# Linear attention on one core: two stores of the first pair moved behind the last load

## The chip, the cores and the metric

The kernel runs on one core of a Trainium2 chip. The metric is the device time of one execution in microseconds (us); each time given is that of whole executions, and one further execution was taken with the hardware profiler.

## The reference

Linear attention with the feature map relu(x) + 1, for 8 batches x 12 heads = 96 heads, 512 rows of 64 numbers each, float32 in and out:

```python
Q_feat = np.maximum(0, Q) + 1
K_feat = np.maximum(0, K) + 1
KV = np.einsum('bhkd,bhkv->bhdv', K_feat, V)
K_sum = np.sum(K_feat, axis=2)
numerator = np.einsum('bhqd,bhdv->bhqv', Q_feat, KV)
denominator = np.einsum('bhqd,bhd->bhq', Q_feat, K_sum)
return (numerator / (denominator[:, :, :, None] + 1e-10)).astype(np.float32)
```

Each of Q, K, V and the output has 12.58 MB in float32.

## The kernel before

The heads are handled in six "pairs", s = 0 to 5; a pair is two blocks n = 0, 1 of 128 partitions x 32 rows of 64. For each pair the kernel loads K, V and Q (2 MB of float32 each, turned into 1 MB of bfloat16 by the transfer itself), computes, and stores 2 MB of float32.

The order of work is not left to a scheduler. The dictionary ORDER lists, for every engine, its tasks in the order in which the engine is to run them. A task's name is a letter, the pair, and what part of the pair it is:

- `lv5`, `lk5`, `lq5`: the loads of V, K and Q of pair 5, issued by POOL (line 131). The loads of pairs 0 and 1 are issued ahead of the lists; the very first K block is loaded on SP into a buffer of the output pool (line 124).
- `f50`, `f51`: K's features of the two blocks on DVE (line 147). `v502`: V's block 0, quarter 2, copied into a block diagonal form by DVE or ACT (line 159). `q5`: Q's features on DVE (line 167).
- `k`: the matmuls of features with V and ones (line 178); `e`: their results copied from PSUM by ACT (lines 192 and 196); `t`: transposes of Q's features (line 202); `c`: those copied from PSUM by ACT (line 207).
- `m40` to `m47`: the output matmuls of pair 4 in eight parts (line 219); `n40` to `n47`: for each part a reciprocal and a multiplication on DVE, which write the output tile `o_sb` (lines 235 and 236).
- `s40`, `s41`: the stores of pair 4 in two halves of 1 MB, the first behind n40 to n43, the second behind n44 to n47 (line 138). Pairs 0 to 4 are stored from POOL. Pair 5 is stored from SP as `s50` (1 MB), `s51` and `s52` (half of that each).

What a task waits for is taken from the buffers. K, V and Q have two buffers each, so lv5 waits until all copies `v3..` have read V of pair 3. The output tiles rotate over four buffers, and the first K block took one of them ahead of pair 0; the output tile of pair 4 stands where that of pair 0 stood, and that of pair 5 where that of pair 1 stood. The first norm of pair 4 in DVE's list is n41, the first of pair 5 n50:

```python
return [("om", s, at[0])] + [("st", s - OUT_BUFS, j) for j in stores_of(s - OUT_BUFS)]
```

The parts of the three lists that the text refers to are, in order (DVE's around the last two pairs):

```
DVE  ... q4 f41 n27 n30 n31 n32 n33 f50 n34 v501 n35 f51 n36 n37 v513 v510 n41 n40 q5 n43 n42 ...
POOL ... lk4 lv4 lq4 s00 lv5 lk5 s01 lq5 s10 s11 s20 s21 s30 s31 s40 s41
SP   s50 s51 s52
```

Of the kernel before, what the change touches and what calls it, by code (L numbers as in the profile page):

```python
# [41 lines left out]
        e40 v500 c43 e41 v511 v512 c42 c50 e50 c51 e51 c53 c52  # L42
    """,
    POOL="""
        lv2 lk2 lq2 lv3 lq3 lk3 lk4 lv4 lq4 s00 lv5 lk5 s01 lq5 s10 s11 s20 s21 s30 s31 s40 s41
    """,
    SP="""
        s50 s51 s52
# [371 lines left out]
```

## Time and profile before

| what | value |
|---|---|
| median of 3 runs | 125.86 us (125.64 to 125.92) |
| profiled execution | 125.95 us |
| its span, first to last instruction | 124.2 us |
| busy in the span | DVE 93.5 us (75%), PE 82.6 (67%), ACT 74.3 (60%), POOL 25.2 (20%) |
| read from and written to HBM | 37.75 MB and 12.58 MB |

Busy time is that of the engines' instructions; the DMA engines, sixteen of them, have a row of their own in the slices, and a table of issues with the time from issue to landing. Adding that time to an issue's start gives the moment at which the transfer has landed. A wait for several things is put down to the one that came last by the profile, and where the named engine had long been done, it was another, often a transfer.

### The profile page before, as it was taken

Reading aid. Unit: us, or ns where it says so; the run is one execution under the profiler, and the core shown is the slowest. Engines: PE = TensorE matmul, PEld = TensorE weight load, DVE = VectorE, ACT = ScalarE, POOL = GpSimd, SP = SyncE. Lnnn points to the kernel's source line nnn. Section 1 sums busy time; section 2 is a strip of 40 time slices with the busy share of each in tenths; the row PEclk is TensorE's granted clock in tenths of the full one; section 3 lists DMA queues with packets and bytes.
Section 4 is the critical chain, followed back from the end, with each engine's and each line's share of the span. In section 5 each row is a group of like instructions: output and inputs, shape, how many; then the busy total and the mean of one; then the engine's idle time right before and its main releaser. Section 6 shows DMA issues by size and latency. Waiting matters only on the chain.

```text
span 124.2 us, 2353 instructions
## 1 busy us (share of the span) xinstructions
PE 82.6 (67%) x960; PEld 62.0 (50%) x960; DVE 93.5 (75%) x188; ACT 74.3 (60%) x94; POOL 25.2 (20%) x52
## 2 busy tenths in 40 slices
PE   0000099983999896879439999978577999955000
PEld 0000077862767774568326777856375667633000
DVE  4799963459589696995979799999389999799200
ACT  7538000575756999929991299953999955930000
POOL 6991042000005100073000391202200202020000
PEclk9999999999599999999995999999999999997555
DMA  3999999999999999999999999999999999999992
GB/s 95 333 214 214 215 212 212 215 214 216 214 215 214 212 214 215 215 215 215 215 212 214 215 215 277 310 199 214 277 318 227 389 414 417 416 414 416 408 406 107
DMA packets 8731, 32.13 MB, mean 259 GB/s; under 512 B 528, under 2 KB 528, under 8 KB 8592
## 3 DMA queue, kind: packets, MB, share of 16 engines
q0 software_dynamic: 7504, 28.84, 94.5%
q1 hardware_dynamic: 1216, 3.15, 6.7%
q8 instruction: 7, 0.11, 0.3%
q14 instruction: 4, 0.03, 0.1%
HBM read 37.75 MB, written 12.58 MB: 405 GB/s over the span
## 4 chain that ended last, share of the span: by engine, by line
DMA 39%; DVE 20%; PE 13%; ACT 12%; POOL 6%; issue 2%; POOLq 0%; ACTq 0%
DMA q_raw<-in_Q_dram 20%; DMA k_raw<-in_K_dram 18%; DVE o_sb L236 9%; ACT v_all L159 8%; PE kva_ps L178 7%; DVE kf L147 4%; PE o_ps L219 3%; DVE v_all L159 3%; ACT qt L207 3%; DVE recip L235 2%; DVE qf L167 2%; POOL kva L383 2%; PE qt_ps L202 2%; POOL v_raw L131 2%; POOL q_raw L131 1%
## 5 line engine op out<-in xcount | busy, mean ns | idle before, releaser
L178 PE MATMUL kva_ps<-v_all,kf 128*128 128x260 bf16 x384 | 54.6, 294 | 22.6 <-DVE v_all L159 17.6
L178 PEld LDWEIGHTS <-kf 128*128 128x128 bf16 x384 | 37.4, 104 | 33.2 <-DVE v_all L159 18.2
L159 ACT COPY v_all<-v_raw 32x2048 bf16<-32x2048 bf16 x19 | 36.0, 1896 | 7.6 <-DVE recip L235 3.5
L236 DVE TENSOR_TENSOR o_sb<-o_ps,recip 128x512 f32<-128x512 f32 x48 | 33.2, 692 | 1.7
L207 ACT COPY qt<-qt_ps 128x1024 bf16<-128x1024 bf16 x24 | 23.8, 1014 | 9.4 <-PE qt_ps L202 9.1
L219 PE MATMUL o_ps<-kva,qt 128*64 128x130 bf16 x384 | 20.5, 232 | 5.7 <-DVE o_sb L236 4.1
L147 DVE TENSOR_SCALAR kf<-k_raw,shift,least 128x2048 bf16<-128x2048 bf16 x22 | 16.8, 808 | 9.5 <-PE kva_ps L178 5.2
L159 DVE COPY v_all<-v_raw 32x2048 bf16<-32x2048 bf16 x29 | 20.1, 692 | 0.8
L219 PEld LDWEIGHTS <-qt 128*64 128x64 bf16 x384 | 12.9, 112 | 14.0 <-DVE o_sb L236 5.8
L192 ACT CAST kva<-kva_ps 64x256 bf16<-64x256 f32 x24 | 8.9, 372 | 17.9 <-PE kva_ps L178 17.5
L202 PE MATMUL qt_ps<-identity,qf 128*128 128x128 bf16 x192 | 14.7, 221 | 3.6 <-ACT qt L207 2.5
L202 PEld LDWEIGHTS <-qf 128*128 128x128 bf16 x192 | 12.0, 98 | 5.1 <-issue 2.6
L138 POOL DMA_DIRECT2D out_dram<-o_sb x10 | 8.0, 805 | 30.2 <-DVE recip L235 15.6
L131 POOL DMA_DIRECT2D v_raw<-in_V_dram x7 | 4.8, 684 | 39.7 <-DVE recip L235 18.0
L167 DVE TENSOR_SCALAR qf<-q_raw 128x1024 bf16<-128x1024 bf16 x24 | 8.8, 432 | 5.1 <-DMA q_raw<-in_Q_dram 5.1
L235 DVE RECIPROCAL recip<-o_ps 128x8 f32<-128x8 f32 x48 | 9.6, 201 | 2.6 <-PE o_ps L219 2.3
L131 POOL DMA_DIRECT2D k_raw<-in_K_dram x6 | 4.2, 700 | 12.9 <-DVE kf L147 12.9
L131 POOL DMA_DIRECT2D q_raw<-in_Q_dram x6 | 5.1, 858 | 1.2 <-DVE qf L167 1.2
L261 DVE MEMSET v_all<- 128x2600 f32 x2 | 4.5, 2225 | 1.1 <-issue 1.1
L196 ACT CAST kva<-kva_ps 64x4 bf16<-64x4 f32 x24 | 4.1, 169 | 0.0
L262 ACT COPY v_all<-zero 128x1560 f32<-128x1560 f32 x2 | 2.9, 1488 | 0.0
L147 DVE TENSOR_SCALAR kf<-o_sb,shift,least 128x2048 bf16<-128x2048 f32 x2 | 2.6, 1340 | 0.0
(18 smaller groups left out, 6.6 us busy)
## 6 DMA issues: line engine op xcount, KB each, us to landing
out_dram<-o_sb POOLq DMA_DIRECT2D x10, 1024.0 KB, 22.5
q_raw<-in_Q_dram POOLq DMA_DIRECT2D x6, 1024.0 KB, 23.9
k_raw<-in_K_dram POOLq DMA_DIRECT2D x5, 1024.0 KB, 19.5
v_raw<-in_V_dram POOLq DMA_DIRECT2D x5, 1024.0 KB, 18.3
o_sb<-in_K_dram SPq DMA_DIRECT2D x1, 1024.0 KB, 4.9
v_raw<-in_V_dram POOLq DMA_DIRECT2D x2, 512.0 KB, 8.6
out_dram<-o_sb SPq DMA_DIRECT2D x1, 1024.0 KB, 8.5
out_dram<-o_sb SPq DMA_DIRECT2D x2, 512.0 KB, 7.5
```

The source lines that it names most:

```text
L131: nc.gpsimd.dma_start(out=t[:, ns[0] : ns[-1] + 1], in_=drams[x][:, 2 * s + ns[0] : 2 * s + ns[-1] + 1])
L138: engine.dma_start(out=o_dram[:, 8 * s : 8 * s + 8][:, ms], in_=outs[s][:, ms], single_packet=engine is nc.gpsimd,)
L147: nc.vector.tensor_scalar(out=kf[:, :, a], in0=raw["k", s, n], scalar1=shift[:, a : a + 1], scalar2=least[:, a : a + 1], op0=ALU.add, op1= ...
L159: copy(out=v_alls[n][ps, :, b * D : b * D + D], in_=raw["v", s, n][ps])
L167: nc.vector.tensor_scalar(out=qf[:, :, cs, n], in0=rows[:, :, cs], scalar1=1.0, scalar2=1.0, op0=ALU.add, op1=ALU.max,)
L178: nc.tensor.matmul(kva_pss[s, n], lhsT=kfs[s, n][:, c].rearrange("p a d -> p (a d)"), rhs=v_alls[n][:, c], start=(c == 0), stop=(c == ROWS ...
L192: nc.scalar.copy(out=kva[po, a::2, n, 0:D], in_=kva_ps[pi, 0 : 4 * D].rearrange("p (b d) -> p b d", b=4),)
L202: nc.tensor.transpose(qt_ps[:, c, r], qfs[s][:, r, 2 * i + c], identity)
L207: copy(out=qts[s][:, 2 * i : 2 * i + 2], in_=qt_pss.pop((s, i)).rearrange("p c r q -> p c q r"),)
L219: nc.tensor.matmul(o_ps[64 * t : 64 * t + 64, c // 2, (c % 2) * W : (c % 2) * W + W], lhsT=qts[s][:, 4 * i + c, 16 * k : 16 * k + 16], rhs ...
L235: nc.vector.reciprocal(out=recip, in_=cells[:, :, :, :, D:D1])
L236: nc.vector.tensor_tensor(out=outs[s][:, e + 2 * u :: 4, 4 * i : 4 * i + 4].rearrange("p n (b c) d -> p b c n d", b=2), in0=cells[:, :, :, ...
```

## The change

In POOL's list, s00 and s01, which stood between lq4 and lv5 and between lk5 and lq5, are placed behind lq5. Nothing else is touched: the same instructions with the same tiles are issued, on the same engines.

```diff
     POOL="""
-        lv2 lk2 lq2 lv3 lq3 lk3 lk4 lv4 lq4 s00 lv5 lk5 s01 lq5 s10 s11 s20 s21 s30 s31 s40 s41
+        lv2 lk2 lq2 lv3 lq3 lk3 lk4 lv4 lq4 lv5 lk5 lq5 s00 s01 s10 s11 s20 s21 s30 s31 s40 s41
     """,
```

## The prediction

> **What bounds the kernel now.** I read the page's slices first, then the chain, then the transfers one by one with their landings, and last the timelines of POOL, SP and DVE around the moved stores.
>
> The slices of the page: each digit is the busy share of a fortieth of the span (3.1 us), the numbers are GB/s.
>
> ```profile
> DVE  4799963459589696995979799999389999799200
> DMA  3999999999999999999999999999999999999992
> GB/s 95 333 214 214 215 212 212 215 214 216 214 215 214 212 214 215 215 215 215 215 212 214 215 215 277 310 199 214 277 318 227 389 414 417 416 414 416 408 406 107
> ```
>
> No compute engine is full throughout, but the DMA engines are, from the second slice to the last but one. The rate has two levels: about 214 GB/s for loads (counted as bf16 written, so twice that is read) and about 415 for stores. Between them, in slices 25 to 31, the two moved stores stand among the loads of the last pair.
>
> The chain of waits tells another story: its last piece is DVE's last norm, and before it come ACT, PE and DVE without a break from 62.8 us on.
>
> ```profile
> 114.85 0.69 DVE o_sb L236
> ```
>
> It ends at 115.5 us, 8.7 us short of the span's end. So I ask what happens after it: the issues of the SP queue, from DMA queries over 112:117, with the time from issue to landing in the last column.
>
> ```profile
> out_dram<-o_sb SPq DMA_DIRECT2D x1, 1024.0 KB, 8.5
> out_dram<-o_sb SPq DMA_DIRECT2D x2, 512.0 KB, 7.5
> ```
>
> The last store, s52, is asked for at 115.6 and takes 7.7 us, landing at 123.3. Its neighbour s51 (asked for at 114.73, 7.3 us) lands at 122.0, so the bytes of s52 need 1.3 us; the other 6.4 us it stands behind older stores. On the page the very first K load, on the same queue with next to nothing ahead, took 4.9 us for 1024 KB from issue to landing. The slack of the last store therefore lies between 7.7 - 4.9 = 2.8 and 7.7 - 1.3 = 6.4 us. The end is set by bytes waiting at the DMA engines, not by the chain.
>
> **The two moved stores.** POOL's timeline around them, then its DMA issues between 69.5 and 73.2 us in the order of time (last column again issue to landing).
>
> ```profile
> 55.08 0.73 POOL L131 DMA_DIRECT2D q_raw<-in_Q_dram  x1
> 55.78 1.10 POOL L138 DMA_DIRECT2D out_dram<-o_sb  x1
> 70.32 0.70 POOL L131 DMA_DIRECT2D v_raw<-in_V_dram  x1 [13.43 <-issue]
> 71.02 0.72 POOL L131 DMA_DIRECT2D k_raw<-in_K_dram  x1
> 71.73 0.79 POOL L138 DMA_DIRECT2D out_dram<-o_sb  x1
> 72.50 0.79 POOL L131 DMA_DIRECT2D q_raw<-in_Q_dram  x1
> ```
>
> ```profile
> v_raw<-in_V_dram POOLq DMA_DIRECT2D x1, 1024.0 KB, 15.3
> k_raw<-in_K_dram POOLq DMA_DIRECT2D x1, 1024.0 KB, 19.5
> out_dram<-o_sb POOLq DMA_DIRECT2D x1, 1024.0 KB, 21.3
> q_raw<-in_Q_dram POOLq DMA_DIRECT2D x1, 1024.0 KB, 25.4
> ```
>
> Start plus last column is the landing: v5 at 85.6, k5 at 90.5, s01 at 93.0, q5 at 97.9. The same query for q4 (55.08 + 22.4) and s00 (55.78 + 24.5) gives 77.5 and 80.3. Transfers of POOL's queue land in the order of issue, one after the other: a load alone costs 90.5 - 85.6 = 4.9 us, a store 93.0 - 90.5 = 2.5.
>
> **The change part by part.** Nothing is added or removed: ten stores and the same loads still go through POOL, with 2 x 1 MB of stores behind lq5 instead of among the loads.
>
> *POOL's own time.* lv5 is held until 70.32 by the release of its buffer: DVE's copies for the third block of V end at 69.8. That stays. With s00 gone from 55.78, POOL idles 14.5 us instead of 13.4. Then lv5, lk5, lq5 go out at 70.3, 71.0 and 71.7, s00 and s01 at about 72.5 and 73.3 (0.8 us each by the rows at 71.73 and 73.29), s10 at about 74.1 instead of 73.29, s11 0.8 later too. These wait in the queue for 27 us and more anyhow; s20, asked for at 78.06, is far behind them. Cost 0, hidden by that backlog.
>
> *Does the queue run dry without s00?* q4 lands at 77.5, v5 is asked for at 70.3: 7.2 us of transfers stand ahead. Cost 0; it would begin to cost if lv5 were released after about 76.
>
> *The loads.* Counting on from 77.5: v5 lands at 82.4 (3.2 us earlier), k5 at 87.3 (3.2), q5 at 92.2 (5.7).
>
> *The two stores.* s00 lands at 94.7 (14 us later), s01 at 97.2 by nominal durations, or 97.9 if the sum of these five transfers stays as measured. From s10 on (100.5) the queue stands where it stood. This is the main term: the same five transfers between 77.5 and 97.9, in another order, 0 us.
>
> *Compute.* DVE's timeline shows whom the earlier loads free:
>
> ```profile
> 87.38 0.69 DVE L236 TENSOR_TENSOR o_sb<-o_ps,recip 128x512 f32<-128x512 f32 x1
> 90.56 1.53 DVE L147 TENSOR_SCALAR kf<-k_raw,shift,least 128x2048 bf16<-128x2048 bf16 x2 [2.50 <-DMA k_raw<-in_K_dram]
> 99.42 0.69 DVE L236 TENSOR_TENSOR o_sb<-o_ps,recip 128x512 f32<-128x512 f32 x1
> ```
>
> The 2.50 us wait of f50 for k5 goes (87.3 is before 88.1, when DVE is free). ACT's wait of 3.50 us before v502, ended at 85.75, is put down to DVE's recip, but v5 landed at 85.6, so that also shrinks to about 0.5. Compute of the last pair moves 2.5 us forward.
>
> *A wait added.* The line at 99.42 is n41, the first norm of pair 4. Its output tile takes the buffer of pair 0 (four rotate, and the first K load took one), so it waits for s00 and s01 to land. Before, s01 was in at 93.0 and n41 did not wait. Now it would come at 99.42 - 2.5 = 96.9 and waits until 97.2 to 97.9: 0.3 to 1.0 us. Behind it on DVE stand n40, q5, n43 and all the rest; PE's m42 and later m's wait for the psum they free, and t50 for q5. Net, DVE still runs 1.5 to 2.2 us earlier.
>
> *What that buys.* s52 would be asked for 1.5 to 2.2 us earlier and find the same bytes ahead of it: it waits 1.5 to 2.2 us longer. Gain 0.
>
> The sum: 0 on the profiled execution (span 124.2, 125.95 with what lies around it). The median of the runs shown is 125.86, 0.09 below, and the forecast is put on it.
>
> **Rivals.** *Faster: alternating between stores and loads costs engine time, and three of the four changes of kind go.* From q4 to v5, s00 + v5 took 85.6 - 77.5 = 8.1 us where 2.5 + 4.9 = 7.4 are nominal: 0.7 too much. From k5 to q5, s01 + q5 took 97.9 - 90.5 = 7.4: nothing too much. So the price is between 0 and 0.7 for the first alternation and 0 for the second. A landing is that of the slowest of 16 engines, and a hiccup of some of them in one execution looks the same; one alternation in two without any cost speaks for the hiccup. Time: 125.86 - 0.7 = 125.16 if all of it is systematic and on the engines that end last, 125.6 at a third.
>
> *Slower: the hold at n41 decides.* It does so if s01 lands so late that the last store loses its slack: n41 may start at 99.42 + 2.8 by the lower bound of the slack, 102.2, at no cost. s01 would have to land 4 to 5 us behind 97.9, that is, with two further transfers served ahead of it. At s01 landing with s10's place and s11's (102.9), the price is 102.9 - 102.2 = 0.7: 126.6. The landings in order of issue speak against it.
>
> *Slower: SP's stores meet more of POOL's.* SP's s50 (asked for at 112.21) lands at 120.7. While it was pending, POOL's s40 landed at 104.27 + 11.5 = 115.8 and s41 at 108.92 + 10.1 = 119.0: 3.2 us for s41 in place of 2.5, and then s50 only 1.7 behind. From s31 (98.04 + 15.0 = 113.0) to s50, three stores took 7.7 us against 7.5. So mixing cost 0.2 net, 0.7 if nothing were given back. With s50 asked for up to 2.2 us earlier nearly one more store mixes: another 0.1 to 0.7, and 126.0 to 126.6. I take the lower end, since 1.7 shows the time given back.
> The Trainium skill, page "DMA: Bandwidth & Descriptors", section "Queues, rings and completion order", says that an engine takes turns between the queues it has work for, a whole packet at a time. By that rule mixing only trades one store's delay for another's, and this rival gives 0 on the sum; the pair 3.2 and 1.7 agrees, and nearer to no cost than to 0.7.
>
> *The change does nothing in the trace:* excluded by the timeline, since POOL issues in the order written.
>
> **How the numbers follow.** The forecast (queue full, 0) gets 0.60, with 125.6 to 126.1 as its own range, since the runs shown lie 0.28 apart. Alternation gets 0.22, at 125.2 to 125.6. The n41 hold gets 0.06 and the mixing, above its lower end, 0.12, both at 126.1 to 126.6. A measurement of this kernel can tell about 0.2%, 0.25 us, from no change; so faster 0.22, same 0.60, slower 0.18. The range takes most of the alternation's prices and most of the mixing's: 125.3 to 126.4.
>
> **What would show it.** Right: v5, k5, q5 land near 82.4, 87.3 and 92.2; the slices show a clean step from 214 to 415 GB/s near 92 us with no mixed ones; f50's 2.50 us are gone; n41 waits for a store for up to 1.0 us; DVE's last norm ends 1.5 to 2.2 us earlier while s52 takes about 9.5 us to land; span 124.2. Wrong: a span that follows DVE's end, a DMA row with a digit below 9 between 10 and 120 us, s01 landing far from 97.2 to 97.9, or a stretch from q4's to s10's landing that isn't 23 us.

## The result and the profile after

The changed kernel takes 125.46 us (median of 22 runs, 125.28 to 125.67), the kernel before 125.72 us beside it (22 runs, 125.42 to 126.66). The ratio is 0.9975, 95% interval 0.9964 to 0.9985: 0.25% faster. The time lies in the predicted range, but the forecast "no effect" does not hold, since the interval leaves out 1.

The slices of the changed kernel, as they were shown of before:

```profile
DVE  4799962449589696995969889999999896997000
DMA  3999999999999999999999999999999999999993
GB/s 101 333 215 212 212 215 216 214 214 216 215 212 214 214 216 212 214 218 214 218 215 214 214 214 212 215 212 215 216 314 419 413 421 415 410 417 415 411 409 143
```

The mixed slices are gone: loads at about 214 GB/s run up to slice 29, and within slice 30 the rate steps to about 415. The DMA engines are still busy from one end to the other. DVE ends earlier, in slice 37.

POOL's timeline, and the DMA issues of POOL between 69.5 and 72.3 us (last column: issue to landing):

```profile
55.00 0.72 POOL L131 DMA_DIRECT2D q_raw<-in_Q_dram  x1
70.24 0.72 POOL L131 DMA_DIRECT2D v_raw<-in_V_dram  x1 [14.52 <-issue]
70.95 0.72 POOL L131 DMA_DIRECT2D k_raw<-in_K_dram  x1
71.67 0.72 POOL L131 DMA_DIRECT2D q_raw<-in_Q_dram  x1
72.38 3.35 POOL L138 DMA_DIRECT2D out_dram<-o_sb  x4
```

```profile
v_raw<-in_V_dram POOLq DMA_DIRECT2D x1, 1024.0 KB, 12.1
k_raw<-in_K_dram POOLq DMA_DIRECT2D x1, 1024.0 KB, 16.3
q_raw<-in_Q_dram POOLq DMA_DIRECT2D x1, 1024.0 KB, 20.5
```

Start plus last column: v5 lands at 82.3, k5 at 87.3, q5 at 92.2, against 82.4, 87.3 and 92.2 in the prediction. DVE's timeline at f50 and at n41:

```profile
87.44 0.69 DVE L236 TENSOR_TENSOR o_sb<-o_ps,recip 128x512 f32<-128x512 f32 x1
88.05 1.62 DVE L147 TENSOR_SCALAR kf<-k_raw,shift,least 128x2048 bf16<-128x2048 bf16 x2
97.36 0.69 DVE L236 TENSOR_TENSOR o_sb<-o_ps,recip 128x512 f32<-128x512 f32 x1 [0.41 <-DMA out_dram<-o_sb]
```

f50 no longer waits; n41 now waits 0.41 us for a store. The chain of waits, whose first line below starts at s01's issue (73.36) and ends at its landing, 97.24, goes through that wait and ends with DVE's last norm at 113.48, 2.1 us earlier than before:

```profile
73.36 23.88 DMA out_dram<-o_sb
97.24 0.03 issue
97.27 0.05 DVEq L236
97.32 0.04 issue
97.36 0.69 DVE o_sb L236
...
112.79 0.69 DVE o_sb L236
```

And the stores of SP, which land at the end:

```profile
out_dram<-o_sb SPq DMA_DIRECT2D x1, 1024.0 KB, 9.9
out_dram<-o_sb SPq DMA_DIRECT2D x2, 512.0 KB, 8.9
```

s51 and s52 are asked for 2.1 us earlier and take 8.9 us (the middle of the two) in place of 7.5. So 1.4 of the 2.1 us were given back, as the queue is still full; 0.7 us were not. The span went from 124.2 to 123.5 us. Compute came early exactly as worked out, and the DMA engines were faster by 0.7 us in these two executions, 0.26 us in the medians.

Where? Each landing has 16 signals in the trace, and the last of them counts. q4's last signal came at 77.52 us before and at 77.44 here, s10's at 100.45 (73.29 + 27.2) and at 99.80. From q4 to s10 that is 22.4 us against 22.9, for the same six transfers. From s10 to s52 it is 22.8 us in both. In this pair of profiles the loss of the kernel before lies between q4 and s10.

### The profile page after: what moved, and what is told of

The parts are those of the page before. It is cut to its first block, busy times and chain, and to the rows that moved or that the text cites. A ratio compares the mean times of both kernels' runs of the same rounds, so it can differ in the third digit from the quotient of the medians.

```text
span 123.5 us, 2353 instructions
## 1 busy us (share of the span) xinstructions
PE 82.7 (67%) x960; PEld 62.0 (50%) x960; DVE 93.5 (76%) x188; ACT 74.3 (60%) x94; POOL 25.0 (20%) x52
## 4 chain that ended last, share of the span: by engine, by line
DMA 54%; DVE 13%; ACT 9%; issue 6%; PE 5%; POOL 4%; POOLq 0%; DVEq 0%
DMA q_raw<-in_Q_dram 35%; DMA out_dram<-o_sb 19%; DVE o_sb L236 7%; ACT v_all L159 5%; DVE qf L167 3%; ACT qt L207 2%; PE kva_ps L178 2%; PE o_ps L219 2%; PE qt_ps L202 1%; DVE recip L235 1%; ACT kva L192 1%; POOL v_raw L131 1%; DVE kf L147 1%; POOL k_raw L131 1%; POOL out_dram L138 1%
## 5 line engine op out<-in xcount | busy, mean ns | idle before, releaser
L219 PE MATMUL o_ps<-kva,qt 128*64 128x130 bf16 x384 | 21.0, 235 | 6.7 <-DVE o_sb L236 4.6
## 6 DMA issues: line engine op xcount, KB each, us to landing
out_dram<-o_sb POOLq DMA_DIRECT2D x10, 1024.0 KB, 22.3
```

The costliest lines, as they stand in the source:

```text
L219: nc.tensor.matmul(o_ps[64 * t : 64 * t + 64, c // 2, (c % 2) * W : (c % 2) * W + W], lhsT=qts[s][:, 4 * i + c, 16 * k : 16 * k + 16], rhs ...
```

## What was tested

Three theories at first. **H**: a store ahead of v5's load holds up some of the 16 DMA engines (the 0.7 us between q4 and v5 in the profile of before). **A**: every return from a store to a load costs the same. **C**: the gain comes from compute that ends earlier.

**Half of the change, each half alone, and the order of kinds without the early compute.**

```diff
-lv4 lq4 s00 lv5 lk5 s01 lq5 s10        before
+lv4 lq4 lv5 lk5 s01 lq5 s00 s10        e1_s00_only
+lv4 lq4 s00 lv5 lk5 lq5 s01 s10        e2_s01_only
+lv4 lq4 lq5 lv5 lk5 s00 s01 s10        e3_compute_late
+lv4 lq4 s00 s01 lv5 lk5 lq5 s10        e4_both_ahead
```

> Only s00 is moved behind lq5; s01 stays between lk5 and lq5. The change as a whole gave a ratio of 0.9975 (0.9964 to 0.9985). Theory H (engines lose time where a store stood ahead of v5's load: in the profile of before the slowest of the 16 lost 0.7 us between q4's landing and v5's, none between k5's and q5's): this edit alone gives all of it, 0.9975, and the profile shows q4's to v5's landing at 4.9 us. Theory A (each change between stores and loads costs the same): half, 0.9987. Theory C (the gain comes from compute that ends earlier, not from the DMA order): v5 and k5 land early as with the whole change, so 0.9975 too; e3 tells C from H.

Measured: 1.0007 (0.9990 to 1.0023).

> Only s01 is moved behind lq5; s00 stays ahead of lv5. Theory H: nothing, 1.000, and the profile again shows more than 7.4 us from q4's landing to v5's. Theory A: half of the gain, 0.9987. Theory C: v5 and k5 land as late as before, compute ends as late, 1.000.

Measured: 1.0002 (0.9989 to 1.0016). Neither half alone gives a gain that can be told from 0. H falls with e1, and A fails in both: half the gain, 0.9987, lies below both intervals.

> As the changed kernel, but POOL asks for lq5 ahead of lv5 and lk5. The DMA engines see the same kinds in the same order (three loads, then the stores), but k5 lands at 92.2 us in place of 87.3, so f50 waits until then, later than before the change (90.5), and compute ends some 1.7 us later than before. Theories H and A: ratio to before 0.9975, since only the order of kinds counts. Theory C: no gain, 1.000 or above.

Measured: 0.9974 (0.9963 to 0.9985). Its DVE timeline at f50 and at the last norm, then SP's issues:

```profile
92.27 1.54 DVE L147 TENSOR_SCALAR kf<-k_raw,shift,least 128x2048 bf16<-128x2048 bf16 x2 [3.54 <-DMA k_raw<-in_K_dram]
117.21 0.69 DVE L236 TENSOR_TENSOR o_sb<-o_ps,recip 128x512 f32<-128x512 f32 x1
```

```profile
out_dram<-o_sb SPq DMA_DIRECT2D x1, 1024.0 KB, 5.6
out_dram<-o_sb SPq DMA_DIRECT2D x2, 512.0 KB, 4.5
```

f50 waits 3.54 us and compute ends at 117.9, 4.4 us later than in the changed kernel and 2.4 later than before, and the whole gain is there. C falls. So compute may end at least 2.4 us later than in the kernel before at no cost; the slack of its last store was put at 2.8 to 6.4.

> s00 and s01 both ahead of lv5, so one stretch of 2 MB of stores between q4 and v5, and loads without a break after it. Theory H: the loss at v5 stays, 1.000. Theory A: one change of kind to stores and back is gone of two, 0.9987. Theory C: v5 and k5 land 2.5 us later than before and compute ends later: 1.000 or above.

Measured: 1.0012 (0.9994 to 1.0030): no part of the gain, with both stores in one stretch.

So it is the order of kinds at the DMA engines, and not their number of changes: one store or two, one return or two, all give the time of before.

**More returns, the cut alone, another place, and the kernel before once more.** Theory S kept the price on returns, but let the slowest engine's delay add up only a little; F put it on the first store of the kernel; P on what else runs at 75 to 81 us.

```diff
-lk4 lv4 lq4 s00 lv5 lk5 s01 lq5 s10                  before
+lk4 lv4 s00 lq4 s02 lv5 s01 lk5 s03 lq5 s10          e5_four_alternations (512 KB each)
+lk4 lv4 lq4 lv5 lk5 lq5 s00 s02 s01 s03 s10          e6_split_behind      (512 KB each)
+lk4 s00 lv4 lq4 lv5 lk5 lq5 s01 s10                  e7_early_s00
```

> The two stores of pair 0 are cut into four of 512 KB, and one stands between each two of lv4, lq4, lv5, lk5, lq5: four returns from store to load in place of two, the same bytes ahead of q5 as before. Theory S (each return from store to load holds up some of the 16 engines by 0.2 to 0.9 us, unevenly, and the end is that of the slowest engine, so one return costs 0.3 us and more returns add a little): ratio to before 1.001 to 1.003, slow load packets behind every return. Theory F (only the first store of the kernel does it): 1.000, slow packets around the first return alone.

Measured: 1.0006 (0.9986 to 1.0025). By its centre, four returns cost no more than one (1.0007 and 1.0002 above), but the interval does not exclude the 1.001 to 1.003 of theory S. In its packets, those of loads that took over 0.33 us (0.32 is the rule) lie between 69 and 72 us, ahead of the first of the four stores; the later returns show almost none. v4, the load ahead of that store, lands 5.29 us after k4 by the mean of the 16 signals, in place of 4.9 in the changed kernel. That fits theory F, but r1, below, shows slow packets near its second store too, so F is not settled either.

> The control of the one before: the same four stores of 512 KB, all behind lq5. Theories S and F: as the changed kernel, 0.9975. If the cut itself costs something, it shows here.

Measured: 0.9971 (0.9953 to 0.9989): the cut costs nothing, and all behind lq5 the gain is there.

> One return from store to load, but ten us earlier: s00 between lk4 and lv4, landing near 70 us; s01 behind lq5. Theories S and F: the loss of one return, 1.000. Theory P (the loss at 75 to 81 us belongs to what compute or POOL do there): none, 0.9975.

Measured: 1.0017 (0.9999 to 1.0036). P falls: at another place the loss is there too.

> The kernel before, unchanged: a second profile of it, and what two equal kernels differ by. All theories: 1.000. If the 0.7 us lost between q4's and v5's landing was a chance of one execution, load packets near 81 us are not slow here; by S and F they are again.

Measured: 1.0001 (0.9981 to 1.0020). Its profile again has slow load packets near 75 and 81 us, and near 94 too. The 0.7 us between q4 and v5, though, are not there: by POOL's starts and its landings, q4 came at 55.05 + 22.9 = 78.0 and v5 at 70.66 + 14.7 = 85.4, 7.4 us in all. From q4 to s10 the last engine took 22.9 us again. The loss of the slowest engine thus falls between other transfers from one execution to the next, and what a pair of landings shows of it is chance.

**Form of the stores, queue, or writing to HBM.** M: writes to HBM among reads from it cost 0.3%, once. K: the form of POOL's stores. Q: any break in POOL's stream of loads.

```diff
-            single_packet=engine is nc.gpsimd,
+            single_packet=engine is nc.gpsimd and s > 0,     e8_many_packets (order of before)
```

> The kernel before, with the order of before, but the two stores of pair 0 without the single_packet option, so that the order of kinds stays and only the form of the stores changes. Theory M (HBM writes among HBM reads cost 0.3 to 0.5 us at the slowest engine, once, however many there are): 1.000. Theory K (it is the form of POOL's stores, one packet for each engine, that breaks the stream of loads): 0.997.

Measured: 1.0003 (0.9980 to 1.0025). K falls as far as this option goes; the trace lists the same 7040 packets of 4 KB on POOL's queue with and without it, so it does not show that the form of the stores changed.

```diff
+    def copy_aside():
+        nc.gpsimd.dma_start(out=scratch, in_=outs[0][:, 0::2], single_packet=True)
...
+lk4 lv4 lq4 x00 lv5 lk5 lq5 s00 s01      e9_copy_among   (x00: the copy)
+lk4 lv4 lq4 lv5 lk5 lq5 x00 s00 s01      e10_copy_behind, e14_copy_behind
+lk4 x00 lv4 lq4 lv5 lk5 lq5 s00 s01      e13_copy_early
+lk4 lv4 x00 lq4 lv5 lk5 lq5 s00 s01      e15_copy_mid
+lk4 lv4 s00 lq4 lv5 lk5 lq5 s01          e16_store_mid   (no copy)
```

> The changed kernel (s00, s01 behind lq5) with one more transfer that the result does not use: 1 MB of pair 0's output copied from SBUF to SBUF, on POOL's queue ahead of lv5, where s00 stood. It adds its own time in this kernel and in its control, so the two are compared with each other. Theory M: equal to the control, since nothing is written to HBM among the loads. Theory Q (any transfer of another kind in the stream of loads costs this): 0.003 above the control.

> The control of the one before: the same copy behind lq5. An estimate from the change's rows, a store of the same size at 2.5 us: ratio to before 0.9975 + 0.020 = 1.017, and by theory M the same in the run before, by theory Q 1.020 there.

Measured: 1.0183 (1.0141 to 1.0224) and 1.0173 (1.0134 to 1.0212). The difference, 0.001, can't be told from 0 nor from 0.003.

> The changed kernel once more, beside the same runs of the kernel before as the other three, and for a second profile. All theories: 0.9975; by M no load packet is held up between the landings of q4 and of k5.

Measured: 0.9980 (0.9957 to 1.0002). The centre agrees with the first comparison; this interval alone would not exclude 1. Much as M has it, none of POOL's packets between 74 and 82 us took over 0.33 us, in this profile as in the first one of the changed kernel; in the two profiles of the kernel before 20 and 14 did.

> The added copy from SBUF to SBUF now between lk4 and lv4, where a single store gave 1.0017 (0.9999 to 1.0036); both stores of pair 0 behind lq5. Theory M: equal to its control. Theory Q: 0.003 to 0.004 above it.

> The control of the one before, run beside it: the same copy behind lq5; it was at 1.0173 (1.0134 to 1.0212). Theories M and Q: 1.0175.

Measured: 1.0214 (1.0189 to 1.0239) and 1.0178 (1.0159 to 1.0197): 0.0036 apart by their centres, as Q has it, though with 6 and 4 runs the two intervals overlap a little. The stretch in which k4 is loaded, just ahead of the copy, first of e13, then of its control (busy time of PE, PEld, DVE, ACT and POOL, then PE's clock, the DMA engines' busy share and their rate in GB/s):

```profile
64.00:67.00 3.00, 2.35 (x20) 1.64 (x21) 2.93 (x7) 1.71 (x2) 0.00 (x0) 0.76 1.03 208
```

```profile
64.00:67.00 3.00, 2.48 (x17) 1.51 (x18) 2.93 (x7) 1.54 (x2) 0.00 (x0) 0.50 1.08 217
```

208 against 217 GB/s would be 27 KB in these 3 us, but the same view has 215 and 209 GB/s, the other way round, for 62 to 64 us, so the rates alone show little. The packets show more. In e13, 26 of POOL's packets between 64 and 68 us took over 0.33 us, 5.8 us in all above 0.324 each; in the control none did. By the mean of its 16 signals k4 lands 5.30 us after k3 in e13 and 4.91 in the control. So loads are held up just ahead of the copy, with no write to HBM anywhere near.

> The added copy from SBUF to SBUF at a third place, between lv4 and lq4; both stores of pair 0 behind lq5. With the copy behind lq5 the ratio was 1.0178 (1.0159 to 1.0197). Theory M (writes to HBM needed): 1.018. Theory Q (any break in POOL's stream of loads costs): 1.021.

Measured: 1.0186 (1.0159 to 1.0214): by its centre 0.001 above the control, again not to be told from either theory.

> The store s00 at the same place, s01 behind lq5. Theories M and Q: the loss of one break, 1.000 to 1.002. If the place decides, 0.9975.

Measured: 1.0040 (1.0019 to 1.0061), 0.0065 above the changed kernel: by its centre, a store at this place costs more than at the other places on POOL's queue, and more than M or Q expected.

```diff
-SP   s50 s51 s52
+SP   s00 s50 s51 s52          e11_s00_on_SP   (POOL: lq5 s01 s10)
+SP   s00 s01 s50 s51 s52      e12_both_on_SP  (POOL: lq5 s10)
```

> s00 is asked for by SP as soon as its four norms are done (near 40 us), on SP's own queue, so that POOL's queue holds an unbroken stream of loads; s01 stands behind lq5 as in the changed kernel. Theory M (it is writes to HBM among reads from it): the loss is there, 1.000, with slow load packets near 41 us. Theory Q (it is the break in POOL's queue): no loss, 0.9975.

Measured: 0.9999 (0.9987 to 1.0010). The loss is there with POOL's stream of loads unbroken, so a break in it is not needed. (SP's stores go without single_packet, in packets of 2 KB in place of 4, so the queue is not all that differs.) The slow packets that M looked for near 41 us are not there, though. The DMA queries over 38:60 show the store spread thin among the loads:

```profile
out_dram<-o_sb SPq DMA_DIRECT2D x1, 1024.0 KB, 18.1
```

It takes 18.1 us to land, as the loads beside it go on.

> s00 and s01 both from SP's queue, near 40 and 46 us; no store of pair 0 is left on POOL's queue. Theory M: 1.000, since a second store among the loads costs nothing more. Theory Q: 0.9975.

Measured: 1.0033 (1.0014 to 1.0052). M's "nothing more" is wrong for SP's queue: the second store costs another 0.0034. Here s51 and s52 took 4.3 us to land (the middle of the two), a little less than e3's 4.5, and compute ended at 119.4, so some of it may be the late compute.

**What all profiles together show.** Each transfer's landing is told by 16 signals, as many as there are DMA engines, and they are taken here as one from each. The table has s52's, counted from the mean landing of v3 (ahead of anything moved), as mean of the 16 and as the last, for one profiled execution each:

```
                        mean    last   (us since v3's mean)
after                   69.90   70.61
r2_after                69.87   70.83
e3_compute_late         69.92   70.57
e6_split_behind         69.88   70.69
before                  70.13   71.15
r1_before               70.06   71.01
e1_s00_only             70.00   70.98
e2_s01_only             70.02   70.96
e4_both_ahead           70.17   71.00
e5_four_alternations    70.20   71.17
e7_early_s00            70.02   70.84
e8_many_packets         69.95   70.79
e16_store_mid           69.95   71.43
e10 / e14 copy_behind   72.37 / 72.37   73.26 / 73.17
e9 copy_among           72.39   73.15
e13 copy_early          72.74   73.87
e15 copy_mid            72.58   73.80
```

With the loads unbroken the last engine ends at 70.57 to 70.83. With a store of POOL's among them it ends at 70.79 to 71.43 (mean of the nine: 71.04, against 70.68 for the four): 0.36 us. The mean over the engines differs by 0.16 us, from 69.89 to 70.06. e16 weighs in this: without it the last engine's difference is 0.31 us. So about half of the loss is work held up, and the other half is unevenness between the engines. The end of the kernel is the last engine's.

The held-up packets account for the mean. Between 62 and 95 us, POOL's packets that took over 0.33 us cost 5.5 and 3.5 us in all above 0.324 each in the two profiles of the kernel before, and 1.1 and 0.6 us in the two of the changed kernel. Shared by 16 engines, the difference is 0.23 us on average, beside 0.21 between the means of these four rows.

e11 and e12 are not in the table, since their stores land beside the loads around v3. Counted from v2's mean landing, s52's mean comes at 84.66 to 84.72 us in the four with unbroken loads, at 85.05 in e11 and at 85.68 in e12. On SP's queue the loss is thus in the mean too.

Beside the stores, the unevenness has a source that is in every profile alike:

```profile
q8 instruction: 7, 0.11, 0.3%
```

These seven transfers of 16 KB on a queue for instructions take 0.89 to 1.18 us each. In the profile of the changed kernel the first one starts at 31.50 us, and of q1's signals one then trails their mean by 1.20 us, where at v1 none trailed by more than 0.2. In r1 the last signal trails by 0.65 us at q5 and by 1.11 at s10, and between the two such a transfer ran (97.50 to 98.48 us). Which engines the stores and which the instruction transfers hit was not controlled. How the uneven half divides between them stays open. That the price doesn't grow with the number of POOL's stores fits a maximum over engines; this too is argued and not shown.

What stays open is what holds the engines up. The early copy (e13) speaks against the need of a write to HBM, by its held-up packets more than by its ratio. At the two other places for the copy the ratios leave it undecided, and the packets over 0.33 us just ahead of the copy were 18 (e15, 2.9 us in all above 0.324 each) and 5 (e9, 0.5 us). SP's store (e11) says that a break in POOL's queue is not needed. What they have in common is transfers of another kind sharing the engines with the loads; a single mechanism behind them was not found.

## Why the prediction was wrong

*POOL, the queue, the loads.* Right: lv5 was held until 70.24, the queue never ran dry, and the three loads landed within 0.1 us of the forecast.

*Compute and the added wait.* Right: f50's 2.50 us went, n41 waited 0.41 us (0.3 to 1.0 forecast), and DVE's last norm ended 2.1 us earlier (1.5 to 2.2).

*What that buys.* Right: nothing. e3 ends compute 4.4 us later than the changed kernel and loses none of the gain.

*The two stores: "the same five transfers between 77.5 and 97.9, in another order, 0 us."* This is the step that failed. With s10 they took 22.4 and 22.5 us in the two profiles of the changed kernel, and 22.9 in both of the kernel before: the term put at 0 was about 0.5 us of the last engine's time here, and 0.26 us in the medians. The prediction had named a stretch that isn't 23 us as a sign of being wrong. The bytes and the order of service were right, but the term took it that an engine needs the same time for a transfer whatever stands beside it. e1, e2, e4 and e7 show about 0.3% for any store among the loads; e3 and e6 show none without. The stretch is not the place of the loss in every order: in e4 and e8 it takes 22.3 us, and the last engine's delay lies ahead, in q4's landing, 25.9 us after v3's mean in both, in place of 25.4 in the changed kernel.

*The rival that alternation costs engine time* had the right sign, and the time, 125.46, lies within its 125.2 to 125.6. It got 0.22 for a reason that was wrong. That s01 with q5 took exactly its nominal 7.4 us was taken to mean that the 0.7 us at the first break was "a hiccup". By r1 the 0.7 us between q4 and v5 was indeed chance in its place, but the loss itself is, by the centres, in every comparison of the two orders. And by e1 and e2 one break costs as much as two, so a second break without a cost was no evidence against a price. It would have been better to compare the whole stretch, q4's to s10's landing, with its nominal sum, 3 x 4.9 + 3 x 2.5 = 22.2 us: the 22.9 of before was 0.7 too much, of which the change took away 0.5.

*The other two rivals.* The hold at n41 did not decide. The mixing with SP's stores took place, with 9.9 us for s50 to land in place of 8.5, and no loss between s10 and s52: 22.8 us in both kernels.

## What to carry to other kernels

When the DMA engines are busy from end to end, moving compute may buy nothing, as here, but the order of kinds in the queue still can: an unbroken stream of loads and then the stores was worth 0.25%, and on POOL's queue one store among the loads cost about as much as two. Sum up a saturated stretch against the nominal times of its transfers and ask for the remainder, rather than take "same bytes" for "same time". The end is the slowest engine's, so a disturbance that is uneven over the engines costs more than its mean, in these profiles about twice.

## What was not expected of the hardware

- A copy from SBUF to SBUF, 1 MB, among loads from HBM held up the load just ahead of it in one place (e13: 5.30 us between two landings in place of 4.91), and went with 0.36% on the kernel by the centres.
- A transfer of 16 KB of instructions made one of the 16 landing signals about 1 us late (1.20 us behind the mean at q1 in the changed kernel), and the lag was still 0.91 us at the next landing.
- The loss at a store is not additive on POOL's queue (1.0002 to 1.0017 in e1, e2, e4 and e7 with one or two, 1.0006 with four halves), but on SP's queue the second store cost about as much as the first (0.9999, then 1.0033).
- A store placed between lv4 and lq4 (e16) cost 0.65% against the changed kernel, at the other places on POOL's queue 0.27 to 0.42%; why was not found. e5 has a store of half the size at this place and cost 0.31%. In e16's profile the mean over the engines is only 0.05 us above that of the changed kernel, and the last engine 0.82: its lag grew from 0.90 us at v4 to 1.71 at s00, and between the two an instruction transfer ran (73.23 to 74.20 us).
